# A first token chunk that comes by channel, and projection weights in larger pieces

## The chip, the cores and the metric

The kernel runs on one core of a Trainium2 chip. The metric is the device time of one execution in microseconds (us), the median of several runs; less is better. A core has five engines that each work through a queue of their own in a fixed order: TensorE (PE in the profile, its weight loads PEld), VectorE (DVE), ScalarE (ACT), GpSimd (POOL) and SyncE (SP), which here issues all DMAs. They wait for each other by semaphores.

## The reference

One gated-DeltaNet layer and one latent-attention layer over 16 learned meta tokens and 1024 input tokens of width 1024, all in float32. Only the head of the first layer matters here:

```python
h = rms_norm(x, g_norm)          # x * rsqrt(mean(x*x) + eps) * g, per token
z = h @ w_in                     # 1024 -> 4112: queries, keys, values, gates, and 16 columns
qkv = silu(causal_dwconv(z[..., :2 * DN_KW + DN_VW], conv_w))    # four taps per channel
beta = sigmoid(b_raw)            # b_raw and a_raw are the last 16 columns of z
g = -exp(a_log) * softplus(a_raw + dt_bias)
```

What follows (the delta rule chunk by chunk, the output projection, the shared keys and values, attention, its output projection) isn't touched by the change.

## The kernel before

All of the layer's matmuls contract over channels, so the normalised input is held with channels on partitions: `hT_hi` and `hT_lo`, 128 partitions x 8 blocks (`kt`) x 1040 tokens. A float32 value is kept as a sum of two values in a shorter float32 form that the matmul takes in one pass, and a product is three matmuls, hi by hi, hi by lo, lo by hi (`mm3`, lines 90 to 93). Splitting is two operations: a copy that rounds (the hi part) and a subtraction (the lo part); for weights `split_w` does the first on POOL and the second on DVE (lines 98 and 99), for PSUM results `split_ps` does them on ACT and DVE (lines 110 and 111).

The 1040 tokens are cut into three chunks (`TOKC`): chunk 0 has 272 tokens (16 meta tokens and the x tiles 0 and 1), chunks 1 and 2 have 384 each (the tiles 2 to 4 and 5 to 7). For each chunk, in turn, the tokens come with tokens on partitions (`xt`, DMA of line 221); ACT squares a tile and sums along it (line 82, `ss`), `rsqrt` (lines 173 to 178) makes the factor with three small DVE operations around two small ones of ACT, POOL scales the tile into `xs` (line 252), PE transposes it block by block (line 258), and `split_ps` takes the result from PSUM to `hT`, multiplied by the norm's gain. The gains are columns of `pcol`: nine small DMAs bring parameter rows into `prow`, PE transposes them once (line 237), and DVE copies them (line 238).

Behind that stand two users of `hT`. The 16 last columns of the projection (`wab`, L274 and L275 into `fin`, 16 matmuls per chunk) give beta and g; g (line 318) is needed by four matmuls at L325 to L328. The projection itself goes in blocks of 128 output channels (`load_w`, `gemm_T`, `conv_acts`): two DMAs of 256 KB into `raw` (line 203), the split, 24 matmuls for each chunk (`mm`), a copy of the result by ACT (`z`, line 370), the convolution on POOL and DVE (`kn`, lines 372 and 375). The first two blocks are keys of heads 0 and 1.

The program is written in this order, but a scheduler sets the order on each engine when the program is built, from the dependencies and its own costs; at run time each queue is fixed. SP too works in order: a DMA that waits for a buffer holds up those behind it, and a DMA waits until the eighth before it has landed.

## Time and profile before

| | |
|---|---|
| median of 3 runs | 1351.07 us (1346.55 to 1354.87) |
| the profiled execution's own time | 1351.8 us |
| its span in the profile | 1350.1 us |
| PE busy | 1306.3 us, 97% of the span |
| DVE, ACT, POOL busy | 67%, 40%, 31% |

The profile is of one execution. Its own time is 1.7 us longer than the span, which starts with the first recorded instruction and ends with the last. A row of the timeline gives the start in us, the busy time, the engine, the line, the operation and the tiles (out<-in), and in brackets the idle time before it and what ended it. Names are without buffer numbers, so `tr` is any of three PSUM tiles and `xs` any of the scaled tiles.

### The profile page before, as it was taken

The page shows a single profiled execution, that of the slowest core. Times are in us where ns is not written, and L with a number is a line of the kernel's source. Part 1 is how long each engine was busy: PE and PEld are TensorE (multiplying, and loading weights), DVE is VectorE, ACT ScalarE, POOL GpSimd, SP SyncE. Part 2 cuts the span into 40 slices and gives each one's busy share as a digit, 9 for nine tenths or more (in the row PEclk, how much of TensorE's full clock was granted, in tenths as well). Part 3 has the DMA queues.
Part 4 walks back from the last instruction along what each step waited for, and adds up shares of the span by engine and source line. Part 5 has one row for each costly group of instructions (what it writes and reads, how often), then busy time and mean ns, then how long its engine had stood idle before and what let it go on. Part 6 is the DMA issues. An engine that isn't in the chain of part 4 may idle for free.

```text
span 1350.1 us, 24895 instructions
## 1 busy us (share of the span) xinstructions
PE 1306.3 (97%) x9064; PEld 1181.7 (88%) x9064; DVE 900.1 (67%) x2601; ACT 534.8 (40%) x1694; POOL 412.8 (31%) x680
## 2 busy tenths in 40 slices
PE   6999999999999999999999999998999999998998
PEld 4879989989998999997888798887999999998876
DVE  6669879968978884633553765224888878788221
ACT  6442343244325322211222243116777677776100
POOL 3344224323421320060101402212535435347000
PEclk9999999999999999999999999999999999999999
DMA  6111202111211113255441302311111101014443
GB/s 185 41 25 48 56 20 62 40 42 37 59 49 32 50 32 96 72 159 178 145 147 68 95 1 84 121 47 57 44 38 35 56 21 36 21 36 149 133 124 125
DMA packets 116924, 96.81 MB, mean 72 GB/s; under 512 B 28462, under 2 KB 106094, under 8 KB 116802
## 3 DMA queue, kind: packets, MB, share of 16 engines
q1 hardware_dynamic: 116802, 95.23, 23.7%
q8 instruction: 71, 1.16, 0.4%
q14 instruction: 51, 0.42, 0.1%
HBM read 68.19 MB, written 27.01 MB: 71 GB/s over the span
## 4 chain that ended last, share of the span: by engine, by line
PE 75%; DVE 8%; DMA 5%; POOL 5%; ACT 4%; issue 3%; SPq 0%; DVEq 0%; ACTq 0%; POOLq 0%
PE mm L91 7%; PE mm L93 7%; PE mm L92 7%; PE sc L93 6%; PE sc L92 6%; PE sc L91 6%; PE bd L91 3%; PE bd L93 3%; PE bd L92 3%; PE pt L1312 2%; PE tr L483 1%; DMA raw<-in_a_w_out 1%; ACT junk L82 1%; DMA out<-raw 1%; PE ch L625 1%
## 5 line engine op out<-in xcount | busy, mean ns | idle before, releaser
L91 PE MATMUL mm<-hT_hi,whi 128*128 128x384 f32 (+1 forms) x768 | 256.8, 334 | 3.5 <-DVE whi L98 3.5
L93 PE MATMUL mm<-hT_hi,wlo 128*128 128x384 f32 (+1 forms) x768 | 255.3, 332 | 0.7 <-DVE wlo L99 0.7
L92 PE MATMUL mm<-hT_lo,whi 128*128 128x384 f32 (+1 forms) x768 | 255.7, 333 | 0.0
L91 PEld LDWEIGHTS mm<-hT_hi,whi 128*128 128x128 f32 x768 | 147.4, 192 | 5.5 <-issue 4.7
L93 PEld LDWEIGHTS mm<-hT_hi,wlo 128*128 128x128 f32 x768 | 147.5, 192 | 2.5 <-DVE wlo L99 1.3
L92 PEld LDWEIGHTS mm<-hT_lo,whi 128*128 128x128 f32 x768 | 147.2, 192 | 1.4 <-issue 0.4
L108 DVE TENSOR_TENSOR pTl<-pt,pTh 128x256 fp32r<-128x256 f32 (+2 forms) x112 | 55.0, 494 | 11.0 <-ACT pTh L107 9.5
L98 POOL TENSOR_SCALAR whi<-raw 128x512 fp32r<-128x512 f32 x48 | 37.7, 799 | 70.4 <-PE mm L92 63.8
L82 ACT ACTIVATE P<-P,mx 128x144 f32<-128x144 f32 (+3 forms) x64 | 50.6, 791 | 21.8 <-DVE mx L1270 19.0
L91 PE MATMUL sc<-wo_hi,oTh 128*128 128x512 f32 (+1 forms) x144 | 57.5, 400 | 0.6 <-issue 0.6
L93 PE MATMUL sc<-wo_hi,oTl 128*128 128x512 f32 (+1 forms) x144 | 57.2, 397 | 0.0
L92 PE MATMUL sc<-wo_lo,oTh 128*128 128x512 f32 (+1 forms) x144 | 56.9, 395 | 0.0
L375 DVE SCALAR_TENSOR_TENSOR kn<-z,pcol,kn 128x384 f32<-128x384 f32 (+1 forms) x72 | 41.4, 576 | 19.4 <-POOL kn L372 18.8
L1283 POOL TENSOR_SCALAR P<-P,sl 128x144 f32<-128x144 f32 (+3 forms) x64 | 53.0, 829 | 3.7
L370 ACT COPY z<-mm 128x384 f32<-128x384 f32 (+1 forms) x72 | 31.8, 442 | 54.4 <-PE mm L93 54.3
L107 ACT CAST pTh<-pt 128x256 fp32r<-128x256 f32 (+2 forms) x112 | 47.3, 427 | 14.1 <-PE pt L1312 8.0
L99 DVE TENSOR_TENSOR wlo<-raw,whi 128x512 fp32r<-128x512 f32 x64 | 47.1, 746 | 8.5 <-POOL whi L98 8.4
L93 PE MATMUL sc<-h_hi,wlo 128*128 128x512 f32 x128 | 50.8, 397 | 0.0
L92 PE MATMUL sc<-h_lo,whi 128*128 128x512 f32 x128 | 50.6, 396 | 0.0
L91 PE MATMUL sc<-h_hi,whi 128*128 128x512 f32 x128 | 50.5, 395 | 0.0
L91 PE MATMUL bd<-wf_hi,oTh 128*128 128x512 f32 x128 | 50.2, 392 | 0.3 <-ACT oTh L1422 0.2
L102 DVE SCALAR_TENSOR_TENSOR wlo<-raw,pcol,whi 128x128 fp32r<-128x128 f32 x64 | 23.4, 429 | 40.0 <-POOL whi L101 40.0
(380 smaller groups left out, 3951.1 us busy)
## 6 DMA issues: line engine op xcount, KB each, us to landing
raw<-in_a_w_in SPq DMA_DIRECT2D x64, 256.0 KB
xt<-in_x SPq DMA_DIRECT2D x16, 512.0 KB
o_scr<-o SPq DMA_DIRECT2D x64, 64.0 KB
raw<-in_a_w_out SPq DMA_DIRECT2D x8, 512.0 KB
on<-o_scr SPq DMA_DIRECT2D x8, 512.0 KB
x_scr<-xt SPq DMA_DIRECT2D x8, 512.0 KB
raw<-in_b_w_in SPq DMA_DIRECT2D x8, 512.0 KB
gb_scr<-z SPq DMA_DIRECT2D x8, 512.0 KB
```

Source lines behind the costliest of these rows:

```text
L82: i = A.activation(out_ap, in_ap, func, **kw)
L91: TE.matmul(ps, ahi, bhi, start=first, stop=False)
L92: TE.matmul(ps, ahi, blo, start=False, stop=False)
L93: TE.matmul(ps, alo, bhi, start=False, stop=last)
L98: eng.tensor_scalar(out=hi, in0=raw, scalar1=1.0, scalar2=1.0, op0=ALU.mult, op1=ALU.mult)
L99: V.tensor_tensor(out=lo, in0=raw, in1=hi, op=ALU.subtract)
L107: A.copy(hi, ps)
L108: V.tensor_tensor(out=lo, in0=ps, in1=hi, op=ALU.subtract)
L370: A.copy(z[:, 3 + a:3 + b], gemm_T(hi, lo, c))
L375: V.scalar_tensor_tensor(out=yc, in0=z[:, a + j:b + j], scalar=col("cw", 24 * j + m), in1=yc, op0=ALU.mult, op1=ALU.add)
L1283: G.tensor_scalar(out=Pm[:, 0:n], in0=Pm[:, 0:n], scalar1=s, scalar2=1.0, op0=ALU.mult, op1=ALU.mult)
L1312: TE.transpose(pt[:, kb, x * P:(x + 1) * P], Ps[x][0][:, y0 + kb * P:y0 + (kb + 1) * P], ident)
```

## The change: what it does

Chunk 0 comes from the host as a second copy that is already turned: `x_t`, 128 channels x 8 blocks x 272 tokens, in four DMAs of 278 KB (`x0`). Its norm is made without transposes. ACT squares two blocks at a time, DVE adds the two squares (`part`), and PE sums over the partitions with a matrix of ones (L271, full-precision operands, four matmuls into one PSUM bank), so that every partition holds the sum of each token. DVE and ACT make the factor `y` of 272 tokens from it (L273 to L278, six operations on 128 x 272). Then for each block DVE multiplies x by gain and factor (L282), ACT rounds (L283) and DVE subtracts (L284).

For chunks 1 and 2 the sums of three tiles stand in one tile `ss`, and one `rsqrt` makes three factors (`tok_norms`); chunk 1's squares and `rsqrt` are written ahead of chunk 0's blocks. There are six `xt` buffers for six tiles and four `xs` buffers (before: three and five). The parameters come turned from the host (`pcol`, one DMA of 64 KB). The projection weights are re-laid by the host so that a partition's part of a 256 KB DMA is one run of 2 KB instead of four of 512 bytes; `wab` has runs of 512 bytes instead of 64. The first weight block is loaded ahead of chunk 1's tokens, the second behind them; `wab` moves to another pool. Each input is still loaded in full.

```diff
-    off = {}
-    pcol = ctile("pcol", [P, P])
+    pcol = ctile("pcol", [P, COLUMNS])
...
-                SY.dma_start(raw, w_in[:, s4, c0:c0 + P])
+                SY.dma_start(raw, w_in[c0 // P, :, s4])
...
-            xts = {t: load_x(t) for t in (-1, 0, 1)}
...
-            TE.transpose(ptp[:, 0:P], prow, ident)
-            V.tensor_copy(pcol, ptp[:, 0:P])
+            x0 = xp.tile([P, KT, W0], F32, tag="x0", name="x0")
+            sq = xp.tile([P, KT, W0], F32, tag="sq", name="sq")
+            for q in range(0, KT, 2):
+                SY.dma_start(x0[:, q:q + 2], I["x_t"][:, q:q + 2])
+            SY.dma_start(pcol, I["columns"])
+            ready[order[0]] = load_w(order[0])
+            xts = {t: load_x(t) for t in range(2, 5)}
+            SY.dma_start(wab, I["a_w_ab"])
+            xts.update({t: load_x(t) for t in range(5, 8)})
+
+            def tok_norms(tiles):
+
+                ss = xp.tile([P, 3], F32, tag="ss", name=nm("ss"), bufs=2)
+                xss = [xp.tile([P, D], F32, tag="xs", name=nm("xs"), bufs=4) for _ in tiles]
+                for i, t in enumerate(tiles):
+                    act(xss[i], xts[t], AF.Square, accum_out=ss[:, i:i + 1])
+                rsqrt(ss, ss, 1.0 / D, EPS)
+                return ss, xss
+
+            ps = bank("tr", [P, 512])[:, 0:W0]
+            part = xp.tile([P, 4, W0], F32, tag="part", name="part")
+            for i in range(4):
+                q = slice(2 * i, 2 * i + 2)
+                act(sq[:, q], x0[:, q], AF.Square)
+                V.tensor_tensor(out=part[:, i], in0=sq[:, 2 * i], in1=sq[:, 2 * i + 1], op=ALU.add)
+                TE.matmul(ps, ones, part[:, i], start=i == 0, stop=i == 3)
+            sh, y, t = (xp.tile([P, W0], F32, tag=x, name=x) for x in ("xsh", "xy", "xn"))
+            V.tensor_scalar(out=sh, in0=ps, scalar1=-0.5 / D, scalar2=-0.5 * EPS, op0=ALU.mult, op1=ALU.add)
+            act(y, sh, AF.Ln, scale=-2.0)
+            act(y, y, AF.Exp, scale=-0.5)
+            V.tensor_tensor(out=t, in0=y, in1=y, op=ALU.mult)
+            V.tensor_tensor(out=t, in0=t, in1=sh, op=ALU.mult)
+            V.scalar_tensor_tensor(out=y, in0=t, scalar=1.5, in1=y, op0=ALU.add, op1=ALU.mult)
+            first = tok_norms(range(2, 5))
+            for kt in range(KT):
+                f, hi, lo = x0[:, kt], hT_hi[:, kt, 0:W0], hT_lo[:, kt, 0:W0]
+                V.scalar_tensor_tensor(out=f, in0=f, scalar=col("a", kt), in1=y, op0=ALU.mult, op1=ALU.mult)
+                A.copy(hi, f)
+                V.tensor_tensor(out=lo, in0=f, in1=hi, op=ALU.subtract)
+            ready[order[1]] = load_w(order[1])
...
-                for kt in range(KT):
-                    ps = bank("tr", [P, 512])
-                    for xs, r0, k in xss:
-                        TE.transpose(ps[:, r0 - a:r0 - a + k], xs[:k, kt * P:(kt + 1) * P], ident[:k, :k])
+            for c, (a, b) in list(enumerate(TOKC))[1:]:
+                tiles = [t for t in range(NT) if a <= tok(t)[0] < b]
+                ss, xss = first if c == 1 else tok_norms(tiles)
...
+                for kt in range(KT):
+                    ps = bank("tr", [P, 512])
+                    for i, xs in enumerate(xss):
+                        TE.transpose(ps[:, P * i:P * i + P], xs[:, kt * P:(kt + 1) * P], ident)
```

With the change the order of the engines differs in the head alone. On PE the last row that stands elsewhere is a few rows behind g's four matmuls (L325 to L328 before, L362 to L365 with the change), on ACT and DVE about as far; from there on each of PE, DVE, ACT and POOL has the same instructions in the same order. SP issues the same DMAs in the same order from the third weight block on.

PE before, where the `fin` matmuls of chunk 0 end, chunk 1's transposes begin and the first matmuls of a weight block stand (`tr_46` to `tr_48` are blocks 0 to 2 of chunk 1, `xs_29`, `xs_35`, `xs_41` the tiles 2, 3, 4):

```order
L275 MATMUL fin_80_401<-hT_lo,wab_397 32x272
L258 MATMUL tr_46_250<-ident,xs_29_207 128x128
L258 MATMUL tr_47_256<-ident,xs_29_207 128x128
L258 MATMUL tr_48_262<-ident,xs_29_207 128x128
L258 MATMUL tr_46_250<-ident,xs_35_222 128x128
L258 MATMUL tr_47_256<-ident,xs_35_222 128x128
L258 MATMUL tr_48_262<-ident,xs_35_222 128x128
L258 MATMUL tr_46_250<-ident,xs_41_237 128x128
L258 MATMUL tr_47_256<-ident,xs_41_237 128x128
L258 MATMUL tr_48_262<-ident,xs_41_237 128x128
L91 MATMUL mm_95_553<-hT_hi,whi_85_530 128x272
L92 MATMUL mm_95_553<-hT_lo,whi_85_530 128x272
```

PE with the change at the same place (`xs_13`, `xs_14` are tiles 2 and 3; the first rows are the last of 18 `mm` matmuls, blocks 0 to 5 of chunk 0):

```order
L94 MATMUL mm_53_461<-hT_lo,whi_1_104 128x272
L95 MATMUL mm_53_461<-hT_hi,wlo_2_105 128x272
L297 MATMUL tr_23_206<-ident,xs_13_152 128x128
L297 MATMUL tr_24_212<-ident,xs_13_152 128x128
L297 MATMUL tr_25_218<-ident,xs_13_152 128x128
L93 MATMUL mm_53_461<-hT_hi,whi_1_104 128x272
L311 MATMUL fin_46_329<-hT_hi,wab_325 32x272
L312 MATMUL fin_46_329<-hT_lo,wab_325 32x272
L311 MATMUL fin_46_329<-hT_hi,wab_325 32x272
L297 MATMUL tr_23_206<-ident,xs_14_153 128x128
L297 MATMUL tr_24_212<-ident,xs_14_153 128x128
L297 MATMUL tr_25_218<-ident,xs_14_153 128x128
```

Eighteen projection matmuls of chunk 0 now stand ahead of chunk 1's first transposes, and the `fin` matmuls of chunk 0 have moved behind and between them.

DVE before, from the subtraction for `wab` to the factors of tile 2 (`hT_lo` here reads PSUM tiles `tr`):

```order
L99 TENSOR_TENSOR wab_397<-wab,wab_397 128x8x16
L111 SCALAR_TENSOR_TENSOR hT_lo<-tr_25_187,pcol,hT_hi 128x272
L111 SCALAR_TENSOR_TENSOR hT_lo<-tr_26_193,pcol,hT_hi 128x272
L111 SCALAR_TENSOR_TENSOR hT_lo<-tr_27_199,pcol,hT_hi 128x272
L176 TENSOR_TENSOR nt_33_212<-ny_31_210 128x1
L177 TENSOR_TENSOR nt_33_212<-nt_33_212,ns_32_211 128x1
L178 SCALAR_TENSOR_TENSOR ss_30_208<-nt_33_212,ny_31_210 128x1
```

DVE with the change, from the factors of tiles 2 to 4 (`ss_12`) to the second weight block (`x_97` is `x0`, in SBUF, `wlo_20` the second block's lo part):

```order
L179 SCALAR_TENSOR_TENSOR ss_12_151<-nt_18_160,ny_16_158 128x3
L284 TENSOR_TENSOR hT_lo<-x_97,hT_hi 128x272
L282 SCALAR_TENSOR_TENSOR x_97<-x_97,pcol,xy 128x272 x2
L101 TENSOR_TENSOR wab_325<-wab,wab_325 128x8x16
L284 TENSOR_TENSOR hT_lo<-x_97,hT_hi 128x272 x2
L113 SCALAR_TENSOR_TENSOR hT_lo<-tr_23_206,pcol,hT_hi 128x384
L101 TENSOR_TENSOR wlo_20_192<-raw_21_193,whi_19_191 128x512
L101 TENSOR_TENSOR wlo_20_192<-raw_22_197,whi_19_191 128x512
```

The factors of chunk 1 now stand ahead of the end of chunk 0's blocks instead of behind it, and six operations of chunk 0 and of `wab` with both inputs in SBUF stand between them and chunk 1's first subtraction.

DVE before, around g (`wlo_99` is the third weight block's lo part):

```order
L314 TENSOR_TENSOR tt<-tt,mx 128x72
L99 TENSOR_TENSOR wlo_99_647<-raw_100_648,whi_98_646 128x512
L99 TENSOR_TENSOR wlo_99_647<-raw_101_652,whi_98_646 128x512
L317 TENSOR_TENSOR tt<-tt,mx 128x72
L375 SCALAR_TENSOR_TENSOR kn_94_551<-z_93_550,pcol,kn_94_551 128x384
L318 TENSOR_TENSOR g<-tt,nla 128x72
```

DVE with the change, around g:

```order
L351 TENSOR_TENSOR tt<-tt,mx 128x72
L101 TENSOR_TENSOR wlo_57_555<-raw_58_556,whi_56_554 128x512
L394 SCALAR_TENSOR_TENSOR kn_52_459<-z_51_458,pcol,kn_52_459 128x384
L354 TENSOR_TENSOR tt<-tt,mx 128x72
L394 SCALAR_TENSOR_TENSOR kn_52_459<-z_51_458,pcol,kn_52_459 128x384
L355 TENSOR_TENSOR g<-tt,nla 128x72
```

One of the two weight subtractions has gone behind g, and one more `kn` operation stands ahead of it.

More of the change, by code (lines that the diff above doesn't have):

```diff
@@ L40 @@
 PART = count()
+COL = {"a": 0, "kv": 8, "b": 16, "og": 24, "gl": 25, "gq": 27, "kg": 30, "qg": 31, "cw": 32}
+COLUMNS = 128
 TOKC = [(0, 272), (272, 656), (656, 1040)]
@@ L213, in gemm_T, with weights @@
             return ps
+        order = [D, D + P]
+        for h0 in range(0, H, 2):
+            order += [2 * D + h0 * P, 2 * D + (h0 + 1) * P, h0 * P, (h0 + 1) * P]
+            if h0 + 2 < H:
+                order += [D + (h0 + 2) * P, D + (h0 + 3) * P]
+        order += [3 * D + h * P for h in range(H)]
+        ready = {}
+        def weights(c0):
+            n = order.index(c0)
+            for c in order[n:n + 2]:
+                if c not in ready:
+                    ready[c] = load_w(c)
+            return ready.pop(c0)
@@ L234, in body @@
[L234 to L238 removed]
+                xt = xp.tile([P, D], F32, tag="xt", name=nm("xt"), bufs=6)
+                SY.dma_start(xt, I["x"][0, t * P:(t + 1) * P, :])
+                return xt
+            x0 = xp.tile([P, KT, W0], F32, tag="x0", name="x0")
+            sq = xp.tile([P, KT, W0], F32, tag="sq", name="sq")
@@ L342, in body @@
         bp = ld.enter_context(tpool(name="bA", bufs=1))
-        order = [D, D + P]
-        for h0 in range(0, H, 2):
-            order += [2 * D + h0 * P, 2 * D + (h0 + 1) * P, h0 * P, (h0 + 1) * P]
-            if h0 + 2 < H:
-                order += [D + (h0 + 2) * P, D + (h0 + 3) * P]
-        order += [3 * D + h * P for h in range(H)]
-        ready = {}
-        def weights(c0):
-            n = order.index(c0)
-            for c in order[n:n + 2]:
-                if c not in ready:
-                    ready[c] = load_w(c)
-            return ready.pop(c0)
         def conv_acts(c0, tag, bufs):
```

55 lines of the change are left out of this document (19 added, 36 removed).

## The prediction

> **What bounds the kernel now.** I read the page first, for which engine is short of time, then the busy time by stretch for where that engine waits, then PE's timeline of the head, since everything that the change touches lies there.
>
> ```profile
> span 1350.1 us, 24895 instructions
> PE 1306.3 (97%) x9064; PEld 1181.7 (88%) x9064; DVE 900.1 (67%) x2601; ACT 534.8 (40%) x1694; POOL 412.8 (31%) x680
> ```
>
> PE is busy for 1306.3 of 1350.1 us, so at most 43.8 us of the program can be won by ending PE's waits. By stretch (after each length: busy us and instructions of PE, PEld, DVE, ACT, POOL, then granted clock, DMA share, GB/s):
>
> ```profile
> 0.00:10.00 10.00, 1.07 (x3) 0.54 (x3) 4.04 (x19) 5.83 (x13) 4.31 (x13) 1.00 0.52 173
> 10.00:17.00 7.00, 6.62 (x24) 3.79 (x25) 4.04 (x12) 5.34 (x13) 0.59 (x2) 1.00 0.88 241
> 17.00:24.00 7.00, 4.63 (x25) 3.48 (x24) 4.32 (x14) 2.49 (x11) 4.28 (x5) 0.90 0.57 162
> 24.00:30.00 6.00, 6.00 (x39) 5.01 (x39) 4.92 (x10) 4.56 (x11) 0.86 (x2) 0.84 0.59 206
> 30.00:40.00 10.00, 9.67 (x63) 8.06 (x62) 6.24 (x20) 5.58 (x16) 4.45 (x5) 1.00 0.29 76
> 40.00:50.00 10.00, 10.00 (x67) 8.49 (x66) 8.86 (x23) 3.79 (x9) 1.89 (x4) 1.00 0.01 2
> 50.00:60.00 10.00, 9.04 (x59) 8.75 (x58) 5.88 (x13) 4.20 (x11) 5.05 (x10) 1.00 0.18 52
> ```
>
> In the first 24 us PE is busy for 12.32, so 11.7 of its 43.8 idle us lie there; from 24 to 50 us only 0.33. The landmarks on PE:
>
> ```profile
> 8.75 0.45 PE L237 MATMUL tr<-ident,prow 128*128 128x128 f32 x1 [8.75 <-POOL xs L252]
> 10.35 6.41 PE L258 MATMUL tr<-ident,xs 128*128 128x128 f32 x22 [0.53 <-POOL xs L252]
> 16.57 0.41 PE L274 MATMUL fin<-hT_hi,wab 128*32 128x272 f32 x1
> 16.78 0.43 PE L275 MATMUL fin<-hT_lo,wab 128*32 128x272 f32 x1
> 23.13 0.90 PE L258 MATMUL tr<-ident,xs 128*128 128x128 f32 x3 [0.83 <-POOL xs L252]
> 23.71 0.59 PE L91 MATMUL mm<-hT_hi,whi 128*128 128x272 f32 x1
> 29.48 0.49 PE L258 MATMUL tr<-ident,xs 128*128 128x128 f32 x3
> 33.02 0.33 PE L91 MATMUL mm<-hT_hi,whi 128*128 128x384 f32 x1
> 33.19 0.33 PE L92 MATMUL mm<-hT_lo,whi 128*128 128x384 f32 x1
> 36.96 0.55 PE L258 MATMUL tr<-ident,xs 128*128 128x128 f32 x3
> 52.40 0.41 PE L325 MATMUL tr<-g,upto 128*128 128x64 f32 x2 [0.96 <-DVE g L318]
> ```
>
> Chunk 0's channels are ready for their first user at 16.57 (`fin`); the first projection matmul comes at 23.71. Three gates follow: the third tile of chunk 1 is turned at 24.03 (23.13 + 0.90), chunk 1's last block at 29.97, the third tile of chunk 2 at 37.51. At 52.40 come g's matmuls. A few rows behind them the order is that of before on every engine, so the change is worth what it moves this point. A late tile holds PE up directly: its transposes stand in PE's queue with the projection behind them.
>
> **The change part by part.** I follow it from gate to gate. The durations:
>
> ```profile
> L82 ACT ACTIVATE xs<-xt 128x1024 f32<-128x1024 f32 x8 | 8.4, 1054 | 0.2 <-DMA xt<-in_x 0.2
> L252 POOL TENSOR_SCALAR xs<-xt,ss 128x1024 f32<-128x1024 f32 x8 | 8.9, 1120 | 6.6 <-DMA raw<-in_a_w_in 2.3 <-issue 1.6 <-ACT ny L82 1.3
> L375 DVE SCALAR_TENSOR_TENSOR kn<-z,pcol,kn 128x272 f32<-128x272 f32 x6 | 3.3, 547 | 3.6 <-POOL kn L372 3.6
> L82 ACT ACTIVATE kn<-kn 128x272 f32<-128x272 f32 x2 | 0.9, 432 | 0.3 <-DVE kn L375 0.3
> L110 ACT ACTIVATE hT_hi<-tr,pcol 128x384 fp32r<-128x384 f32 x16 | 8.6, 580 | 10.5 <-PE tr L258 10.2
> L99 DVE TENSOR_TENSOR wab<-wab,wab 128x128 fp32r<-128x128 f32 x1 | 0.3, 293 | 0.1
> 27.75 0.68 DVE L99 TENSOR_TENSOR wlo<-raw,whi 128x512 fp32r<-128x512 f32 x1
> 76.17 0.83 PE L440 MATMUL tr<-kn 128*128 128x128 f32 x6
> ```
>
> *Loading.* SP's rows show the issue of the two tiles of chunk 0, the point where SP could go on because the second had landed, and the wait of tiles 2 to 4 for buffers:
>
> ```profile
> 1.24 0.89 SPq L221 DMA_DIRECT2D xt<-in_x  x2
> 6.22 0.22 SPq L231 DMA_DIRECT2D prow<-in_b_q_gain  x1
> 6.92 3.73 SPq L221 DMA_DIRECT2D xt<-in_x  x3
> 4.00:5.00 1.00, 0.00 (x0) 1.00 1.02 418
> ```
>
> 1.09 MB has landed at 6.2. The new `x0` is 1.11 MB, so its last quarter lands at about 6.4 and the earlier ones some 0.7 apart, from 4.3. Behind it come 0.07 MB of columns, 0.52 of weights and three tiles of 0.52; at the 418 GB/s of the last row they land at 6.6, 7.8, 9.1, 10.3 and 11.6. The tiles cost SP no wait any more: six buffers.
>
> *Chunk 0's norm.* No 128 x 544 square is in the trace; between 0.43 (272 wide) and 1.05 (1024) I take 0.65. A 272-wide DVE operation lies between 0.29 (128) and 0.68 (512): 0.45, and 0.5 for the three-operand form (0.547 in the row, some of it held up). The matmul with ones is full precision; L440's, 128 wide, are two instructions each at about 0.11, so 272 wide makes 0.47 on a warm PE, and about 1.8 times that on a cold one (272-wide rows 0.21 apart at 16.57, against 0.12 from the 0.17 between 384-wide rows at 33.02): 0.85. Four of them from 4.3 + 0.65 + 0.45 = 5.4 on end at 8.8. Then the DVE row that scales the sum (9.3), while ACT's logarithm and exponential run to 10.2; but DVE has a small cast (say 0.2) and both weight subtractions (2 x 0.68) queued ahead of the next step, so three more operations of the factor end at 9.3 + 1.6 + 1.4 = 12.3. Four L282 (14.3), two L284 (15.2). From there on PE has projection work: 8.5 us earlier than at 23.71. Two L282, three L284 and four small rows of chunk 1's `rsqrt` bring its factors at 15.2 + 1.0 + 1.35 + 0.65 = 18.2.
>
> *Gate 1, chunk 1 turned.* POOL's three scalings take 3 x 1.12 = 3.36, to 21.6. Behind the factors DVE still has three L284, two L282 and the `wab` subtraction, 1.35 + 1.0 + 0.29 = 2.6. Whether the two run side by side, these rows of POOL and DVE say:
>
> ```profile
> 18.11 0.16 DVE L178 SCALAR_TENSOR_TENSOR ss<-nt,ny 128x1 f32<-128x1 f32 x1
> 18.43 1.12 POOL L252 TENSOR_SCALAR xs<-xt,ss 128x1024 f32<-128x1024 f32 x1 [2.33 <-DMA raw<-in_a_w_in]
> 18.62 0.93 DVE L176 TENSOR_TENSOR nt<-ny 128x1 f32<-128x1 f32 x1
> 20.58 1.12 POOL L252 TENSOR_SCALAR xs<-xt,ss 128x1024 f32<-128x1024 f32 x1 [1.03 <-issue]
> 20.72 0.98 DVE L178 SCALAR_TENSOR_TENSOR ss<-nt,ny 128x1 f32<-128x1 f32 x1
> ```
>
> One-column operations, 0.16 in the first row, end with POOL's instruction (19.55, 21.70): DVE stood still. Both read SBUF twice, as L282 and L284 do, and as `split_ps`, which the change takes out of chunk 0, does not. The Trainium skill says so as a rule ("SBUF — State Buffer", Who interferes with whom): a VectorE instruction with two SBUF inputs and a GpSimd one that reads SBUF exclude each other for a whole instruction. The trace agrees, with 0.93 and 0.98 in place of 0.16.
>
> So the third scaling ends between 21.6 and 18.2 + 3.36 + 2.6 = 24.2. The transposes, the last of them behind `fin` matmuls that need the `wab` subtraction, add 0.4 to 0.8: gate 1 at 22.0 to 25.0. I take about the middle, 23.4, as POOL and DVE will partly alternate: 0.6 earlier than 24.03.
>
> *Gate 2, chunk 2 turned.* Before, 13.48 passed from gate 1 to 37.51. Now two squares of chunk 2 wait for `xs` buffers until chunk 1's last block is turned. From gate 1 to there, as before: 29.97 - 24.03 = 5.94. Then two squares with a 0.58 evacuation between (2.8), the shared `rsqrt` with a copy in between (six small operations of 0.16 to 0.2 with their hand-overs and some 0.55, say 1.8), three scalings (3.36), the transposes (0.4): 8.4, against 7.54 before. I take 13.9, between this sum (14.3) and the 13.48, since PE's cold start behind 23.13 is not all repeated: 0.4 later.
>
> *From gate 2 to g.* Counted in the order, PE has three 272-wide `mm` left where it had five 384-wide: 5 x 0.17 - 3 x 0.12 = 0.5 less. DVE has one weight subtraction less and one `kn` operation more ahead of g: 0.68 - 0.6 (384 wide, so a little over 0.547), about 0.1 off the 0.96 wait. Sum: 0.6 - 0.4 + 0.5 + 0.1 = 0.8 us earlier.
>
> The 24 transposes and the 16 `fin` matmuls of chunk 0 cost nothing or are the same work elsewhere; the column transpose (0.45) lay in PE's wait. With gate 1 at 22.0 and 13.5 behind it, the sum is 2.0 + 0.0 + 0.5 + 1.0 (no wait for g) = 3.5; with 25.0 and 14.3, it is -1.0 - 0.8 + 0.5 + 0.0 = -1.3.
>
> *Larger pieces.* Two 256 KB weight loads alone, by the page of DMA in 40 slices of 0.1 us, and who waited for them in the first 60 us:
>
> ```profile
> GB/s 0 0 0 0 0 0 0 0 0 0 0 77 56 72 118 143 195 230 317 328 343 348 333 318 302 338 343 369 312 261 195 159 67 21 0 0 0 0 0 0
> POOL whi L98 <- DMA raw<-in_a_w_in: 6.6, 2, 4.1
> ```
>
> In runs of 512 bytes they go at about 340 GB/s, token rows at 418, so 0.3 us of 1.5 for a pair may be won. Both waits were POOL's; PE's own idle time in the rows above names `xs` and g alone. Value: 0, between 0 and 0.3 for each of the first two blocks. By the Trainium skill ("DMA: Bandwidth & Descriptors", Specifications) 512 bytes already suffice for full rate; the trace, 340 against 418, doesn't bear that out fully, and the sum is the same by either.
>
> **The rivals.**
>
> *A, the whole head moves up.* POOL goes first and DVE's rest fits beside it: gate 1 at 22.0 and 3.5 us won, 1347.6. For it: PE has 18 projection matmuls done by then. Against: the four rows above.
>
> *B, slower: POOL and DVE take turns.* Each scaling of 1.12 waits for a 0.5 operation of DVE or makes it wait, and chunk 1's subtractions stand behind both; gate 1 at 25.0, 1.3 us lost, 1352.4. It decides from gate 1 later than 24.2. For it: DVE had no two-input SBUF work for chunk 0 before. Against: 24.2 needs full exclusion. The Trainium skill's page on SBUF, named above, makes this exclusion a rule.
>
> *C, the pieces count.* If PE waited for each of the 32 pairs, 32 x 0.3 = 9.6 us, 1341.5. Against: the waits are two, on POOL. This is also how the change would do more than its head.
>
> **How the numbers follow.** The profiled execution took 1351.8; with 0.8 less it is 1351.0, and since it lies 0.7 above the median of the runs, the forecast is 1350.3. Chances: this, from -0.5 to +2.5 won, 0.55; A 0.2; B 0.2; C 0.05. A, B and the forecast all lie from 1347.6 to 1352.4, less than the 8.3 us between the lowest and the highest run before; so the range takes some 3 us on either side from that scatter: 1344.5 to 1355. About 1%, 13.5 us, is what can be told from no change, and more than the 11.7 idle us of the head: within 1% 0.96, faster 0.02, slower 0.02.
>
> **What would show it.** In the changed kernel's timeline the first `mm` should stand at 13 to 16 us, the third tile of chunk 1 be turned at 22 to 25, the third tile of chunk 2 at 36 to 39, g's matmuls start at 49 to 54; DVE rows of L282 or L284 of over 1 us beside POOL's scalings would show the exclusion. The prediction is wrong if g's matmuls come before 48 or after 55, or if the distance from there to the end is not that of before (1297.7) within some 4 us: then something behind the head moved, which I take for the same program.

## The result and the profile after

| | before | changed |
|---|---|---|
| median of 20 runs each | 1351.74 us (1346.55 to 1355.18) | 1343.79 us (1338.77 to 1350.89) |
| ratio | | 0.9948, 95% interval 0.9938 to 0.9959 |
| profiled execution, span | 1350.1 us | 1341.9 us |

The ratio makes the change 5.5 to 8.4 us faster. That is within 1%, as forecast, but the forecast was 0.8 us, and the median lies just under the range of 1344.5 to 1355. The page of the changed kernel shows the same bound as before:

```profile
span 1341.9 us, 24805 instructions
PE 1299.7 (97%) x9047; PEld 1178.1 (88%) x9047; DVE 901.2 (67%) x2588; ACT 533.0 (40%) x1680; POOL 405.9 (30%) x677
```

PE is busy 6.6 us less than before and idle 42.2 us in place of 43.8, so most of the 8.2 us between the two spans is not idle time that went away. Part of it is work that PE no longer has: chunk 0's 24 transposes and the column transpose made 7.5 us of rows before, the sum with the matrix of ones makes 4.00. Part is a faster clock, as the sections below show. The first 60 us by stretch (columns as in the prediction):

```profile
0.00:10.00 10.00, 4.00 (x8) 2.40 (x8) 4.45 (x14) 4.62 (x7) 2.49 (x12) 1.00 0.81 279
10.00:17.00 7.00, 3.50 (x13) 3.03 (x14) 6.90 (x21) 6.60 (x16) 0.69 (x2) 1.00 1.03 400
17.00:24.00 7.00, 6.62 (x42) 5.64 (x42) 5.06 (x9) 3.09 (x9) 5.34 (x5) 1.00 0.15 58
24.00:30.00 6.00, 6.00 (x40) 4.51 (x38) 4.39 (x10) 5.05 (x13) 0.00 (x0) 1.00 0.30 90
30.00:40.00 10.00, 8.70 (x55) 6.71 (x55) 5.03 (x12) 5.04 (x10) 4.34 (x5) 1.00 0.00 1
```

From 10 to 17 us DVE is the busy engine (6.90 of 7 us); from 17 to 30 us PE waits for 0.38 us, where it had waited for 2.37, all of it before 24. The landmarks on PE, and the rows of POOL and DVE around the scalings of chunk 1:

```profile
4.74 4.00 PE L271 MATMUL tr<-part,ones 128*128 128x272 f32 x8 [4.74 <-DVE part L270]
13.00 0.57 PE L93 MATMUL mm<-hT_hi,whi 128*128 128x272 f32 x1 [4.26 <-ACT hT_hi L283]
21.22 0.55 PE L297 MATMUL tr<-ident,xs 128*128 128x128 f32 x3 [0.38 <-POOL xs L292]
34.55 0.55 PE L297 MATMUL tr<-ident,xs 128*128 128x128 f32 x3 [0.55 <-POOL xs L292]
49.81 0.41 PE L362 MATMUL tr<-g,upto 128*128 128x64 f32 x2 [0.74 <-DVE g L355]
```

```profile
11.89 1.77 DVE L282 SCALAR_TENSOR_TENSOR x<-x,pcol,xy 128x272 f32<-128x272 f32 x4
16.40 0.16 DVE L179 SCALAR_TENSOR_TENSOR ss<-nt,ny 128x3 f32<-128x3 f32 x1
16.73 4.44 POOL L292 TENSOR_SCALAR xs<-xt,ss 128x1024 f32<-128x1024 f32 x3 [3.35 <-ACT hT_hi L283]
16.73 1.50 POOL L292 TENSOR_SCALAR xs<-xt,ss 128x1024 f32<-128x1024 f32 x1 [3.35 <-ACT hT_hi L283]
17.24 1.27 DVE L282 SCALAR_TENSOR_TENSOR x<-x,pcol,xy 128x272 f32<-128x272 f32 x1
18.64 1.62 DVE L284 TENSOR_TENSOR hT_lo<-x,hT_hi 128x272 fp32r<-128x272 f32 x2
31.19 3.31 POOL L292 TENSOR_SCALAR xs<-xt,ss 128x1024 f32<-128x1024 f32 x3 [8.85 <-ACT ny L84]
```

(The row of 1.50 is the first of the three scalings in the row of 4.44.) Gate 1 (the third tile of chunk 1 turned) stands at 21.77 in place of 24.03, gate 2 at 35.10 in place of 37.51, g's matmuls at 49.81 in place of 52.40. So 2.6 us are there at g. Right behind g PE has fewer projection matmuls left, and at the matmul at 131.04 us, which stood at 134.26 before, it is 3.2 us. Up to there PE is busy for 116.29 us where it was 118.80: 2.5 of the 3.2 us are less busy time and 0.7 less waiting. The other 5.0 us arise behind that, where both kernels have the same order on every engine.

To find them I took the distance between the same PE instructions in both traces. PE runs in step for long stretches (the shift stays within 0.05 us for 100 us and more) and jumps at few places. Three stages carry what stays the same from trace to trace; all traces of the study stand here, the times of the changed kernel's profile naming the stages. The head runs to a projection matmul at 131 us, the output gate's stage to 650, the attention's output tiles from 1290 to 1330:

| us | 0 to 131 | 131 to 580 | 580 to 650 | 650 to 1253 | 1290 to 1330 |
|---|---|---|---|---|---|
| before | 134.3 | 448.8 | 72.5 | 603.5 | 42.0 |
| e1, before again | 137.2 | 447.4 | 73.7 | 602.5 | 42.2 |
| e9, weights last | 134.7 | 449.1 | 73.3 | 603.5 | 42.8 |
| e3, pieces alone | 134.5 | 447.6 | 72.5 | 602.5 | 41.9 |
| e5, before + 24 | 134.3 | 447.7 | 73.5 | 605.4 | 39.9 |
| changed | 131.0 | 449.0 | 70.0 | 603.0 | 39.9 |
| e8, changed again | 132.1 | 455.0 | 70.2 | 601.4 | 40.2 |
| e2, small pieces | 131.2 | 448.8 | 71.2 | 602.5 | 40.3 |
| e6, changed + 24 | 131.3 | 447.5 | 69.9 | 604.9 | 41.2 |
| e7, third tile on ACT | 130.6 | 447.9 | 70.3 | 603.5 | 39.9 |
| e4, late gate | 137.3 | 452.0 | 70.0 | 602.7 | 40.4 |
| e10, slow gate weights | 131.1 | 448.4 | 73.4 | 601.8 | 40.5 |
| e12, four buffers | 131.0 | 444.4 | 66.6 | 602.3 | 40.8 |
| e11, both | 129.2 | 451.7 | 67.0 | 603.5 | 39.9 |

(1253 to 1290 is 37.1 and the rest 11.8 to 11.9 in all of them.) The head is 3.0 to 3.6 us shorter (the mean of changed, e8, e2 and e6 against that of the old heads, without or with e1), the gate's stage 3.2 (73.3 in the mean of the four with the old head and small pieces, 70.0 in changed, e8 and e6), the output tiles 2.1. The two long stages in between vary by some us either way with the clock: in e8, with 455.0, PE ran at half the clock for 17.07 us in a row at 169.6 us, and why stays open.

*The gate's stage.* The rows of PE in which it waits there, before and after:

```profile
600.69 0.36 PE L91 MATMUL mm<-hT_hi,whi 128*128 128x272 f32 x1 [1.72 <-DVE whi L98]
616.31 0.36 PE L91 MATMUL mm<-hT_hi,whi 128*128 128x272 f32 x1 [1.77 <-DVE whi L98]
```

```profile
596.55 0.36 PE L93 MATMUL mm<-hT_hi,whi 128*128 128x272 f32 x1 [0.64 <-ACT zg L84]
610.75 0.36 PE L93 MATMUL mm<-hT_hi,whi 128*128 128x272 f32 x1 [1.86 <-DVE whi L100]
```

DVE makes `whi` for the last projection blocks, but in its queue the low parts of the output weights (`wo_lo`) stand ahead. These wait for POOL's high parts, and POOL waits for 512 KB loads of `a_w_out`, which stand in one queue with the loads of the projection weights and need one of two buffers that DVE's `wo_lo` has to free first. The same stage by stretch, to the second of those rows and on from it, shows the clock too:

```profile
583.09:616.31 33.22, 29.36 (x170) 28.57 (x169) 14.14 (x14) 3.74 (x8) 15.45 (x11) 0.95 0.50 153
616.31:655.62 39.31, 38.39 (x206) 28.42 (x206) 17.77 (x41) 7.31 (x16) 2.09 (x1) 1.00 0.53 159
```

```profile
580.04:610.75 30.71, 27.86 (x169) 27.05 (x169) 13.38 (x14) 3.75 (x8) 14.76 (x11) 1.00 0.49 165
610.75:650.05 39.30, 38.38 (x206) 28.43 (x206) 18.39 (x41) 7.31 (x16) 1.12 (x1) 1.00 0.53 159
```

Before, 0.95 stands where the changed kernel has 1.00: one stretch of 3.41 us at half the clock, which the trace's clock records put at 602.8 us, 2.1 us behind the end of the first wait. PE is busy 1.50 us longer for it (29.36 against 27.86). All four traces with the old head and small pieces have such a stretch in this stage, and changed, e8 and e6 have none. PE's waits there come to 5.6 us in the mean of the four and to 3.8 in the three. So of the 3.2 us about 1.8 are waiting and 1.4 clock.

*The output tiles.* Each takes one read of `ot_scr`, one of `x1_scr` (`x_scr` in the rows) and one write of `out`; SP issues the next read when the write has landed. Before and after:

```profile
1289.87 0.34 SPq L1430 DMA_DIRECT2D out<-raw  x1
1295.31 0.37 SPq L1418 DMA_DIRECT2D raw<-ot_scr  x1
1301.26 0.32 SPq L1420 DMA_DIRECT2D raw<-x_scr  x1
1301.86 0.34 SPq L1430 DMA_DIRECT2D out<-raw  x1
```

```profile
1283.83 0.34 SPq L1449 DMA_DIRECT2D out<-raw  x1
1286.73 0.37 SPq L1437 DMA_DIRECT2D raw<-ot_scr  x1
1292.72 0.32 SPq L1439 DMA_DIRECT2D raw<-x_scr  x1
1294.70 0.34 SPq L1449 DMA_DIRECT2D out<-raw  x1
```

Before, the third write takes 5.44 us to the next read, and 2.90 with the change; the two writes ahead of it took 2.63 and 2.80. From the late write on the next one is issued 0.6 us behind the read of `x1_scr` (1301.26, 1301.86) and both share the engines, so a tile takes 11.99 us (1289.87 to 1301.86) in place of 10.87. The page of DMA for that one write, in 40 slices (of 0.14 us before and 0.07 us after), shows why, before and after:

```profile
GB/s 447 447 447 387 357 417 298 179 298 387 328 357 387 447 387 387 387 209 60 0 0 0 0 0 30 0 0 30 0 30 30 30 0 30 30 30 0 0 0 0
q8 instruction: 1, 0.02, 1.1%
```

```profile
GB/s 113 621 282 452 395 508 282 565 283 283 283 170 339 113 396 226 565 339 452 452 282 565 282 565 113 678 226 565 339 283 226 226 113 0 0 0 0 0 0 0
q1 hardware_dynamic: 237, 0.84, 70.9%
```

Before, a transfer of instructions (16 KB, at 1292.25) falls into the write. Most of the write is over after 2.5 us, and then single packets of it come one after another for another 2.4 us. In the changed kernel no such transfer is there at that time; it comes 6.9 us behind the write's issue, at 1290.77. The next one, at 1317.85, falls into its sixth write, which then takes 4.41 us to the next read. In all eight traces that have the new head and no spare transposes a transfer falls into the sixth write, and it takes 4.4 to 5.5 us; the writes ahead of it, without one, take 2.6 to 3.2. So the change moved the transfer from the third write to the sixth, behind which fewer tiles are left.

### The profile page after: what moved, and what is told of

Read it like the earlier page. It is cut to its first block, busy times and chain, and to the rows that moved or that the text cites. A ratio compares the mean times of both kernels' runs of the same rounds, so it can differ in the third digit from the quotient of the medians.

```text
span 1341.9 us, 24805 instructions
## 1 busy us (share of the span) xinstructions
PE 1299.7 (97%) x9047; PEld 1178.1 (88%) x9047; DVE 901.2 (67%) x2588; ACT 533.0 (40%) x1680; POOL 405.9 (30%) x677
## 4 chain that ended last, share of the span: by engine, by line
PE 71%; DVE 9%; issue 5%; POOL 5%; ACT 4%; DMA 3%; SPq 0%; ACTq 0%; DVEq 0%; POOLq 0%
PE sc L95 6%; PE sc L94 6%; PE sc L93 6%; PE mm L93 6%; PE mm L94 6%; PE mm L95 6%; PE bd L93 5%; PE bd L95 4%; PE bd L94 4%; PE pt L1331 2%; PE tr L502 1%; PE sc L1284 1%; PE sc L1285 1%; DVE qT L394 1%; PE po L95 1%
## 5 line engine op out<-in xcount | busy, mean ns | idle before, releaser
L110 DVE TENSOR_TENSOR pTl<-pt,pTh 128x256 fp32r<-128x256 f32 (+2 forms) x112 | 54.9, 494 | 11.9 <-ACT pTh L109 10.4
L100 POOL TENSOR_SCALAR whi<-raw 128x512 fp32r<-128x512 f32 x48 | 37.4, 792 | 76.9 <-PE mm L94 71.2
L1300 POOL TENSOR_SCALAR Pe<-P,sl 128x128 f32<-128x128 f32 x64 | 29.5, 462 | 71.3 <-DVE sl L1297 55.2
```

The source lines that it names most:

```text
L100: eng.tensor_scalar(out=hi, in0=raw, scalar1=1.0, scalar2=1.0, op0=ALU.mult, op1=ALU.mult)
L110: V.tensor_tensor(out=lo, in0=ps, in1=hi, op=ALU.subtract)
L1300: G.tensor_scalar(out=Pe, in0=Pm[:, None, 0:NM].broadcast_to([P, E8, NM]), scalar1=s, scalar2=1.0, op0=ALU.mult, op1=ALU.mult)
```

## The experiments

Two theories stood at first. *Clock*: behind the head it is the granted clock, of which the two profiled executions happened to have different amounts (0.989 and 0.992). *Pieces*: the larger weight pieces, which the prediction valued at nothing, shorten the stages behind the head.

**e1: the kernel before, unchanged,** for its clock.

> The kernel before, once more, so that its granted clock is known for every run. In the two profiled executions the changed kernel is 8.2 us shorter: 3.3 of it is there when the projections run behind g's matmuls, the other 4.9 arise where both kernels have the same program. Theory 'clock': the part behind the head is the granted clock (8 dips to 0.5 of 3.41 us in the trace before against 6 after, about 1.5 us each); then the runs of this kernel have a mean clock near 0.987 (the changed kernel's 20 runs: 0.9911, with 9.3 us per 0.01 of clock), ratio 1.000. Theory 'pieces': the larger weight pieces make the rest; then the clock here is 0.991 like that of the changed kernel, ratio 1.000.

1352.82 us, ratio 1.0007 (0.9993 to 1.0021). The mean granted clock was 0.9890, between what the two theories asked for. So about 1.9 us of the medians' difference goes with the clock (0.9911 - 0.9890, at 9.3 us per 0.01, the slope through the changed kernel's 20 runs), not 3.7. Both theories fall as the only cause.

**e2: the changed kernel with small pieces; e3: the kernel before with large pieces.** The layout of the host's array and the address in one DMA differ:

```diff
-                SY.dma_start(raw, w_in[c0 // P, :, s4])      # e2, from the changed kernel
+                SY.dma_start(raw, w_in[:, s4, c0:c0 + P])
...
-                SY.dma_start(raw, w_in[:, s4, c0:c0 + P])    # e3, from the kernel before
+                SY.dma_start(raw, w_in[c0 // P, :, s4])
```

> The changed kernel with its projection weights again in the layout of before, in pieces of 512 bytes; order and work of every engine stay. Theory 'pieces': the 3.7 us that the medians show beyond the head go, 1347.5 (ratio to before 0.997). Theory 'clock': the time stays within 1.1 us of the changed kernel's 1343.8 (ratio 0.995 to 0.996); 1.1 us is the one wait behind the head that was shorter with large pieces, 0.64 in place of 1.72 us ahead of the output projection's weights, near 600 us, and it should be 1.7 again.

> The kernel before with only the projection weights in pieces of 2 KB; head, order and work as before. Theory 'pieces': 3.7 us faster, 1348.0 (ratio 0.997). Theory 'clock': 0 to 1.1 us faster (ratio 0.999 to 1.000), with the wait near 600 us at 0.6 in place of 1.7.

e2: 1345.86 us, 0.9956 (0.9935 to 0.9977). e3: 1350.49 us, 0.9993 (0.9979 to 1.0006). Against the changed kernel e2 is 2.1 us slower by the medians and 1.1 by the ratios, where 'pieces' had 3.7 and 'clock' at most 1.1; against the kernel before e3 is 0.9 us faster by its ratio, where 'pieces' had 3.7. Neither difference is clear of the intervals. The wait near 600 us did as expected: 1.54 us in e2 (due at 1.7) and 0.83 in e3 (due at 0.6); but in e3 the second wait was 2.58 us where before had 1.77. The gate's stage tells it more closely. Its last weight cast on DVE came, counted from the issue of the second load of output weights, at 41.3, 41.1 and 40.9 us with old head and small pieces (before, e1, e5), at 39.8 with old head and large pieces, at 40.0 with new head and small pieces, and at 38.7 to 39.1 with both. So the pieces bring that cast 1.1 to 1.3 us forward with either head, and 1.0 comes with the rest of the change. The stage itself is 1.2 us longer in e2 than in the changed kernel's traces, and 0.8 shorter in e3 than in the mean of the four of before. Rival C had the right sort of mechanism and the wrong place.

**e4: GpSimd scales chunk 1's tiles twice.**

```diff
-                    G.tensor_scalar(out=xss[i], in0=xts[t], scalar1=ss[:, i:i + 1], scalar2=1.0,
-                                    op0=ALU.mult, op1=ALU.mult)
+                    for _ in range(2 if c == 1 else 1):
+                        G.tensor_scalar(out=xss[i], in0=xts[t], scalar1=ss[:, i:i + 1], scalar2=1.0,
+                                        op0=ALU.mult, op1=ALU.mult)
```

> The changed kernel in which GpSimd scales each of chunk 1's three tiles twice (the second pass writes the same values): 3.4 to 4.4 us more on GpSimd ahead of the third tile's transposes. If the head's gates pass on to the end one to one, as the prediction took it, gate 1 stands at 25.2 to 26.2 in place of 21.8 and the time is 1347.2 to 1348.2 (ratio 0.997). If the gain does not come from the gates, the time stays at 1343.8 (0.995).

1348.62 us, 0.9976 (0.9957 to 0.9995): 4.8 us behind the changed kernel by the medians, 0.4 more than the first theory asked at most. Gate 1 came later than I had asked for, since the scheduler put two weight casts between the scalings, and its row stands with a wait of 3.14 us:

```profile
27.91 0.55 PE L298 MATMUL tr<-ident,xs 128*128 128x128 f32 x3 [3.14 <-POOL xs L293]
56.19 0.41 PE L363 MATMUL tr<-g,upto 128*128 128x64 f32 x2 [0.74 <-DVE g L356]
```

The tile is turned at 28.46, 6.7 us behind 21.77, and g's matmuls are 6.4 us late. In that execution 1.1 us of it was there ahead of the scalings already, so the gates pass on to g nearly one to one, and most of it to the end. Some of it is clock: a half-clock stretch of 3.41 us follows the wait at 28.5 us, and in the gate's stage such a stretch cost 1.5 us. The prediction's way from gate to gate holds.

**e5 and e6: 24 spare transposes,** in the kernel before and in the changed one. They were made when the traces had shown the transfer of instructions in the third write.

```diff
+    spare = bank2("bd", [P, 512])
+    for _ in range(24):
+        TE.transpose(spare[:, 0:NM], ident[:NM, :], ident[:NM, :NM])
```

> The kernel before with 24 spare transposes of 16 columns (48 rows of TensorE, whose result nobody reads) in front of the attention stage, near 925 us, where TensorE has 2.6 us of idle time; at most 1.3 us of work. Theory 'instruction load': in all three traces with the old head a 16 KB instruction transfer starts 57.8 to 59.0 us before the end, inside the third write of the output, whose landing then takes 5.0 to 5.4 us in place of 2.9, and from there each output tile takes 11.4 to 11.8 us in place of 10.9; such a transfer comes about every 256 rows of TensorE, so 48 rows move it to about 64 us before the end, into a read. Then the stretch between the last projection of the attention and the end, 1290 to 1330 in the changed kernel's time, takes 40.0 in place of 42.0 us, and the time is 0.7 to 2.0 us shorter (ratio 0.9985 to 0.9995). Theory 'chance': that stretch stays at 42, and the time is 0 to 1.3 us longer (ratio 1.000 to 1.001).

> The changed kernel with the same 24 spare transposes at the same place. Theory 'instruction load': the transfer that started 51 us before the end starts about 56.5 before it, inside the third write of the output; that write takes 5 us in place of 2.9, and the stretch of 39.9 us becomes 41.5 to 42; time 1.6 to 3.3 us longer than the changed kernel, 1345.4 to 1347.1 (ratio 0.9955 to 0.997). Theory 'chance': the stretch stays at 39.9 to 40.4, time 0 to 1.3 us longer.

The same edit moved the transfer out of the write in one kernel and into it in the other. The write and the next read, and the instruction row of the DMA page for the write, of e5 and then of e6:

```profile
1291.61 0.34 SPq L1434 DMA_DIRECT2D out<-raw  x1
1294.46 0.37 SPq L1422 DMA_DIRECT2D raw<-ot_scr  x1
```

```profile
1284.33 0.34 SPq L1453 DMA_DIRECT2D out<-raw  x1
1288.23 0.37 SPq L1441 DMA_DIRECT2D raw<-ot_scr  x1
...
q8 instruction: 1, 0.02, 1.4%
```

2.85 us without it, 3.90 with it, and the stage takes 39.9 us in place of 42.0 in e5, 41.2 in place of 39.9 in e6 (I had asked for 41.5 at least). The theory on the instruction load is right about the stage. On the whole time it was right for e6 (1346.32 us, 0.9959, 0.9942 to 0.9977) and wrong for e5: 1352.41 us, 1.0006 (0.9991 to 1.0020), no gain. The stretch with the spare transposes gave it back (before, then e5):

```profile
918.00:940.00 22.00, 17.37 (x109) 15.31 (x107) 12.20 (x47) 15.76 (x66) 7.01 (x17) 0.92 0.21 64
```

```profile
918.00:940.00 22.00, 18.34 (x105) 16.30 (x104) 10.29 (x36) 13.45 (x54) 3.96 (x10) 0.77 0.19 62
```

The clock there is 0.77 in place of 0.92, 10.24 us at half the clock in place of 3.41. That is of the size of the 1.9 to 2.9 us by which 650 to 1253 is longer in e5. In e6 too the clock is halved for 10.24 us there, and 650 to 1253 takes 604.9 us in place of 603.0. What the edit itself adds there hides what it wins, so the gain of 2.1 us is shown for the stage and not for the whole time.

**e7: the third tile's scaling on ScalarE,** so that GpSimd has two in a row beside VectorE in place of three.

```diff
+                    if i == 2:
+                        A.mul(xss[i], xts[t], ss[:, i:i + 1])
+                        continue
                     G.tensor_scalar(out=xss[i], in0=xts[t], scalar1=ss[:, i:i + 1], scalar2=1.0,
```

> The changed kernel, with the scaling of the third tile of chunk 1 and of chunk 2 on ScalarE in place of GpSimd. If GpSimd's three scalings (4.44 us for chunk 1 where 3.36 are work, the rest given up to VectorE's two-input operations) set the gates, gate 1 comes 1.0 to 1.5 us earlier (20.3 to 20.8 in place of 21.8), gate 2 1.0 to 2.0 earlier (33.1 to 34.1), and the time is at most 1.5 us shorter, since TensorE idles for no more than 1.6 us at these gates. If ScalarE's casts of chunk 0 wait for the scaling instead, TensorE's first projection block gives back what the gates win, and the time stays within 0.5 us of the changed kernel.

```profile
17.43 2.90 POOL L295 TENSOR_SCALAR xs<-xt,ss 128x1024 f32<-128x1024 f32 x2 [3.76 <-DMA dtb<-in_a_dt_bias]
30.95 2.22 POOL L295 TENSOR_SCALAR xs<-xt,ss 128x1024 f32<-128x1024 f32 x2 [9.09 <-issue]
```

GpSimd is done with chunk 1 at 20.33 (21.17 in the changed kernel) and with chunk 2 at 33.17 (34.50). On PE the tiles of chunk 2 are turned at 34.10 (35.10), as the first theory asked, but those of chunk 1 at 21.69 (21.77), since `fin` matmuls stand between their transposes; what went there is PE's wait of 0.38 us. g's matmuls come at 50.15 (49.81), behind a wait of 1.03 us for DVE, and the head as a whole is 0.5 us shorter than in the changed kernel's profile. 1342.31 us, 0.9928 (0.9904 to 0.9952): 1.5 us less, which the interval doesn't tell from none. Beside VectorE a scaling takes 1.45 us (2.90 for two) and without it 1.11 (2.22 for two).

**e8: the changed kernel once more.**

> The changed kernel once more, for its granted clock on the chip of these runs. In the runs so far the clock's mean was 0.9891 for the kernel before (42 runs) and 0.9911 for the changed kernel (20 runs), 1.9 us at 9.3 us per 0.01. Theory 'clock belongs to the program': 0.991 again, ratio 0.995. Theory 'chance': 0.989 to 0.990, and the ratio goes to 0.996, the 6.3 us that remain at equal clock less 1.

1343.79 us, 0.9935 (0.9914 to 0.9957), mean clock 0.9906. The kernel before had 0.9888 to 0.9896 in all of its series. Single runs of the changed kernel spread over 0.986 to 0.997, so e8 alone couldn't decide. Both of its series, 0.9911 and 0.9906, lie above all of those of before, and so 0.001 to 0.002 of clock, 1 to 2 us, goes with the program.

**e9: the weights' array last among the inputs,** in the kernel before.

```diff
+    arrays["a_w_in"] = arrays.pop("a_w_in")
```

> The kernel before; only the host hands over the array of the projection weights as the last of the inputs, as the changed kernel does, so that the arrays lie elsewhere in the chip's memory. Order, sizes and pieces of every engine and transfer stay. In the output gate's stage (580 to 650 us of the changed kernel) the last weight cast of VectorE comes 40.9 to 41.3 us after the second load of that stage's output weights with small pieces and old head, 40.0 with small pieces and new head, 39.8 with large pieces and old head, 38.7 to 39.1 with both; so about 1.0 us there is neither pieces nor anything that the head does. Theory 'place in memory': 40.0 here, and the time 1 us shorter (ratio 0.999). Theory 'something else' (where the instruction transfers fall, for one): 40.9 to 41.3 as before, ratio 1.000.

1351.20 us, 0.9990 (0.9978 to 1.0002); the cast came at 40.8 us and the gate's stage took 73.3. The ratio fits the first theory, but the cast, which was to decide, stayed where it was. So moving this one array does nothing; the places of the others were not tried. The 1.0 us in the gate's stage that is neither this nor the pieces stays open; where the transfers of instructions fall is a candidate that wasn't tried there.

**e10: the low part of the output weights made twice,** to lengthen the two waits of the gate's stage.

```diff
+                last = V.scalar_tensor_tensor(out=w_lo[:, h, :], in0=raw, scalar=col("og"), in1=w_hi[:, h, :],
+                                              op0=ALU.mult, op1=ALU.subtract)
```

> The changed kernel, in which VectorE computes the low part of each block of the output weights twice (same values), 1.28 us more ahead of the casts for which TensorE waits near 597 and 611 us (0.64 and 1.86 us in the changed kernel). In the six traces in which these two waits came to 2.7 us or more, a half-clock stretch of 3.41 us followed at 600 to 618 us; in the five in which they came to 2.4 to 2.8, none did. Theory 'a wait is paid twice': the waits come to 3.9 to 5.1 us, a half-clock stretch follows within 4 us of one of them, and the stretch of 70.0 us (580 to 650) becomes 73.0 to 74.3. Theory 'wait alone': 71.3 to 72.7, no half clock there. The time follows: 1346.8 to 1348.1, or 1345.1 to 1346.5.

```profile
598.68 0.36 PE L93 MATMUL mm<-hT_hi,whi 128*128 128x272 f32 x1 [3.30 <-DVE whi L100]
600.39 0.59 PE L95 MATMUL mm<-hT_hi,wlo 128*128 128x272 f32 x1 [1.22 <-DVE wlo L101]
...
597.00:608.00 11.00, 8.10 (x37) 7.91 (x38) 9.88 (x10) 0.40 (x1) 3.23 (x2) 0.69 0.74 238
579.51:614.27 34.76, 30.23 (x170) 29.73 (x170) 23.12 (x22) 3.25 (x7) 16.01 (x11) 0.90 0.43 137
```

The waits came to 4.5 us, all ahead of one block, and a clock of 0.69 stands where the changed kernel had 1.00. The stage took 73.4 us. Up to its second block it is 34.76 in place of 30.71 us, with PE idle for 1.68 us more and, at the lower clock, busy for 2.37 more (30.23 against 27.86); behind that it is 0.65 shorter, 0.36 of it a wait for `wlo` that is gone. So here a wait of PE was paid again in clock, as the first theory said. The whole time, 1346.24 us (0.9970, 0.9956 to 0.9984), lies in the other theory's range; the mean clock of these runs was 0.9885.

**e11 and e12: four buffers for the output weights' pieces,** e11 together with e7.

```diff
-            rp = lr.enter_context(tpool(name="wr", bufs=2))
+            rp = lr.enter_context(tpool(name="wr", bufs=4))
```

> The changed kernel with both: the third tiles scaled on ScalarE as in the run before, and four buffers in place of two for the output weights' pieces, so that their loads no longer wait for VectorE. If the gate stage's waits come from that chain, the 0.64 and 0.36 us waits at 597 go, the one of 1.86 at 611 shrinks to 0 to 1, and the time is 1.5 to 2.5 us below that of the run with ScalarE alone: 1340 to 1341 (ratio 0.9915 to 0.992). If the loads of the projection's weights, which now come behind more of the output weights, are late instead, the waits stay at 2 to 3 us and the time at 1342.

> The changed kernel with the four buffers alone. As above: 1341.5 to 1342.3 (0.9925 to 0.993) if the waits go, 1343.8 (0.994) if they stay.

Both waits go altogether. The first part of the stage in e12 (its profile is of the fastest of six runs), with PE idle for 0.26 us in place of 2.85:

```profile
575.45:603.44 27.99, 27.73 (x169) 27.28 (x169) 17.72 (x16) 3.26 (x7) 16.88 (x11) 1.00 0.48 163
```

The stage takes 66.6 and 67.0 us, 3.0 to 3.4 less. e11: 1340.81 us, 0.9919 (0.9907 to 0.9931), as its first theory asked, and the lowest median of this study, of five runs: its interval lies below that of the changed kernel's 20 runs (0.9938 to 0.9959), while that of e8 (0.9914 to 0.9957) still overlaps it. e12: 1342.94 us, 0.9932 (0.9911 to 0.9953), between what its two theories asked for, though the waits went. In the whole time the buffers show as 0.9 us (e12 against the changed kernel) and 1.5 us (e11 against e7), which the intervals don't tell from none.

## Why the prediction was right, and where it was wrong

- *Within 1%: right,* with the sign. The reason, that the head has only 11.7 idle us to give, covers the head alone, and that gave 3.2 of the 8.2 us between the profiles. The rest was put at nothing, and that it stayed small enough is luck. The size was 0.8 us against 5.5 to 8.4.
- *Loading and chunk 0's norm: right at its end, by two errors that cancel.* The first matmul of the sum started at 4.74 and not at 5.4, and the four took 4.00 us and not 3.4; the sum was due at 8.8 and is read from PSUM at 8.77. The factor was due at 12.3 and is there at 11.85. The first projection matmul stands at 13.00, at the edge of the 13 to 16 of the signs and 2.2 us ahead of the 15.2 of the working, as it waits for the first rounded block alone.
- *Chunk 1's factors at 18.2: this step failed, by 1.6 us.* They are there at 16.56 (16.40 + 0.16). An L282 took 0.44 (1.77 for four) and not 0.5, an L284 0.39 and not 0.45, chunk 0's factor came 0.45 earlier, and the four small rows of `rsqrt` cost next to nothing between the others. With it gate 1 (21.77) fell ahead of the 22 to 25 that were to show the forecast, and gate 2 (35.10) ahead of 36 to 39.
- *From the factors to gate 1: right in its length.* I had 5.2 us, about the middle between 3.8 and 6.8, and 16.56 to 21.77 is 5.2; that the middle is hit so closely is luck. The sign of the exclusion came: an L282 takes 1.27 us beside a scaling in place of 0.44, and the first scaling 1.50 in place of 1.11. Each of the three scalings waits for an operation of DVE (4.44 us and not 3.36) and DVE then waits for it. This agrees with the Trainium skill's rule ("SBUF — State Buffer", Who interferes with whom); e7 shows the price, 1.45 us a scaling against 1.11. So the turn-taking of rival B is there. Its gate at 25.0 is not, as the factors came 1.6 us earlier and the scalings lost 1.1 us, not the whole 2.6 of DVE's queue.
- *Gate 2 and g: nearly right.* 13.33 us from gate to gate, where I had 13.9 and before 13.48. From gate 2 to g's matmuls it is 0.2 us less, and the rest of the 0.6 that I had comes right behind them, where the matmuls that are gone would have stood: to the matmul at 131 it is 0.8 to 0.9 less. So the head wins 3.0 to 3.6 us, the size of rival A (3.5), which had 0.2, but not by A's mechanism: POOL does not go undisturbed.
- *"A few rows behind them the order is that of before on every engine, so the change is worth what it moves this point": this is the step that made most of the error.* The order is the same, the time isn't: from g's matmuls to the end it is 1292.1 us and not 1297.7, outside the bound that the prediction had set, and 5.0 of these 5.6 us lie behind the matmul at 131. Three things that no order shows account for most of it: the size of the pieces where loads compete (1.1 to 1.3 us in the gate's stage, valued at 0), the place at which PE's instructions are fetched relative to the output's writes (2.1 us), and the clock, which falls behind waits of PE (1 to 2 us by its means, 1.4 of it within the gate's stage). One us of the gate's stage stays open.
- *Larger pieces.* I had looked at the two waits in the first 60 us alone. Their price had to be read where PE waits for weights at all, and that is near 600 us: its two rows of 1.72 and 1.77 us were in the trace of before. That 512 bytes suffice, which the Trainium skill's page on DMA says ("DMA: Bandwidth & Descriptors", Specifications), isn't borne out where transfers compete here: by e2 and e3 pieces of 2 KB bring the last cast of the gate's stage 1.1 to 1.3 us forward.

## What to carry to other kernels

That the order behind a change is the same doesn't make its time the same: look there for the places where the bound engine waits at all, and ask of each what a transfer that lands earlier, later or in larger pieces does to it. Such a wait can cost more than its length, since the clock may fall behind it. In the traces here two more buffers shortened a stage that the change did not touch by 3.0 to 3.4 us, as much as the new head wins in the head, though no difference of that size shows in the whole time yet. A difference of under 1% should be taken apart by the distance between the same instructions in several traces before it is put down to a cause.

## What the runs showed of the hardware

- *Instructions are fetched through the same DMA engines.* About every 256 rows of PE, matmuls and weight loads together, a 16 KB transfer comes (71 for the 18128 rows of the program before). When it falls into a write of 512 KB, one part of that write ends up to 2.6 us late, and a chain with no slack keeps losing 0.5 to 1.1 us per tile. Whether it hits depends on how many instructions stand ahead: 24 spare transposes moved it in and out.
- *The clock halves for 3.41 us at a time, on a grid, and behind waits shorter than that.* In each trace all such stretches start a whole number of 3.413 us apart (before at 22.6, 128.4, 264.9 and 602.8, for instance: 31, 71 and 170 of them from the first), and where this grid lies against the program differs from execution to execution (the first one comes at 22.6 us before and at 24.3 in e1). In the gate's stage seven traces have a stretch, and it follows a grid period in which PE stood still for 1.7 to 2.9 us. No period with 1.6 us or less is followed by one there; one with 1.77, at 613.1 us before, isn't either. The sum of PE's two waits does not tell it: 2.74 us in e2 with a stretch, 2.75 in e7 without. The period ahead of the stretch at 602.8 before, and the stillest one of the changed kernel's stage (length, then PE's busy time):

```profile
599.39:602.80 3.41, 1.75 (x12) 1.57 (x13) 3.41 (x5) 0.10 (x1) 1.94 (x1) 1.00 0.51 119
606.90:610.31 3.41, 1.99 (x12) 1.67 (x10) 2.39 (x3) 0.49 (x1) 1.82 (x1) 1.00 0.35 140
```

  So whether a wait of 2 us is paid again depends also on how it falls on the grid. In the head a stretch comes at 22 to 25 us in all five traces with the old order (PE waiting 2.37 us of 7) and in e4 behind the wait of 3.14, and between 20 and 120 us in none of the eight other traces with the new head, whose single waits there are under 1.1 us. The Trainium skill ("TensorE: Matmul & The Clock Gate", HAM oscillation — how this bites in real kernels) sets the point at idle gaps of about 3.4 us; here a gap of 1.72 us was enough (before, at 600.69).
- *It also halves where PE doesn't wait.* Near 250 and 267 us almost every trace has one or two such stretches (e12 has none), though in the changed kernel PE is busy for 79.95 of the 80 us up to 250. No run here shows why.
